# Two decoder blocks on one core: distance in SBUF between moving and next stationary operands, 256 to 448 bytes modulo 512

## The chip, the cores and the metric

The kernel runs on one core of a Trainium2 chip. The metric is the device time of one execution in microseconds (us). Three executions of the kernel before took 3676.75, 3681.95 and 3683.27 us, with a median of 3681.95 us.

## What is computed

The reference runs a residual stream x of 256 tokens by 1024 channels through two blocks, each of two layers, all in float32. A layer of the first block is a mixer, an expert layer and a gate:

```python
xn = rmsnorm(h, norm_mix[l])
z = xn @ w_in[l]                                   # 1024 x 9728
# attention with a window of 128, a short convolution and a gated recurrence, then
y = jnp.einsum('nbsw,nwd->nbsd', branches, w_branch[l])
h = h + jnp.einsum('bsnd,nbsd->bsd', g, y) @ w_out[l]
h = h + peer(rmsnorm(h, norm_ffn[l]), w_peer_q[l], peer_sub_keys[l], peer_u[l], peer_v[l])
h = h + jax.nn.sigmoid(rmsnorm(h, norm_ple[l]) @ w_ple_gate[l]) * (p[l] @ w_ple_proj[l])
```

`peer` picks 16 of 16384 experts for each of 8 heads and token. The kernel computes it densely: all products of the tokens with `peer_u`, a sparse gate, and a product with all of `peer_v`. A layer of the second block projects to 10272 columns, runs a gated delta rule in both directions beside a differential attention, and projects back twice.

## The kernel before, in words

All activations stay in SBUF, channels on the partitions and 256 tokens along the free dimension. Weights come from HBM in pieces of 1 MB into one of three `raw` buffers.

**How a product is made precise.** Most of the products are done in float32r, a float32 form that TensorE takes in one pass, and each operand is split in two: a high part (ScalarE, L167) and the rest (VectorE, L170). `mm3` (L196 to L200) then issues three products for each 128x128 piece of weights: high weights by high x (L198), high weights by low x (L199), low weights by high x (L200). The weights are the stationary operand: 128 columns of float32, 512 bytes in each partition. x is the moving operand: 256 tokens, 1024 bytes in each partition. Every product has a weight load (PEld) of its own.

**Who uses it.** `proj` (L202) calls `mm3` 16 times for 256 output columns, 48 products. `add_rows` (L338) calls it for row blocks of a weight matrix. In the expert layer `u_split` (L902) calls it with rows of `peer_u` as the weights. `v_pair` (from L930, products on L943) turns the roles: activations `ah` and `al` are stationary, 512 columns of split `peer_v` rows (`whi`, `wlo`) are moving. `proj_tok` (L216, products on L226 to L228) also turns them: x is stationary, the weights are moving, 256 columns.

**Products in plain float32.** `u_whole` (L888, products on L898) and the router's projection (L762) use unsplit float32. The profile shows two passes for each of these.

**Where the tiles lie.** Tile pools are placed one after the other in SBUF, in the order in which they are opened: `const`, `state` (the tiles x), `ring` (`raw`, and the split weights `whi` and `wlo`), then the pools of a stage, which are closed and give way to the next stage's: `zp` for the first block's mixer (its split activations are `bh` and `bl`), `peer` (`ah`, `al`), `ple` (`ph`, `pl`, and four weight buffers of its own), `zp2` for the second block's mixer (`bh`, `bl`). `shift(pool, size)` (L75) allocates a dummy tile of `size` bytes in each partition, first in its pool, so that all later tiles of that pool, and of the pools opened after it, lie `size` bytes higher. Nothing reads or writes the dummy. The sizes are `SHIFTS` (L36, one for each layer) and the ring's (L65). The pieces of x within a tile lie 1024 bytes apart and the pieces of weights 512 bytes, so the distance from a moving operand to the stationary one that is loaded meanwhile is the same modulo 512 throughout a stage.

**Order.** The order of instructions on each engine is set when the program is built, by a scheduler with priorities. All weights are issued from SyncE's queue.

Of the kernel before, what the change touches and what calls it, by code (L numbers as in the profile page):

```python
# [32 lines left out]


URGENT = 3000
SHIFTS = {"zp": (320, 96), "zp2": (192, 192), "ple": (192, 448), "peer": (256, 256)}  # L36
SQ_ACT = (2, 5, 7)
HPOOL = ()
WPOOL = 0
# [2 lines left out]
class Tiles:  # L42


    def __init__(self, tiles):
        self.tiles = tiles
# [5 lines left out]
class Ctx:  # L52
# [6 lines left out]
    def __init__(self, ctx, tc):  # L59
        self.tc = tc  # L60
        self.nc = tc.nc
        self.const = ctx.enter_context(tc.tile_pool(name="const", bufs=1))
        self.state = ctx.enter_context(tc.tile_pool(name="state", bufs=1))
        self.ring = ctx.enter_context(tc.tile_pool(name="ring", bufs=1))
        self.shift(self.ring, 256)  # L65
        self.ps = ctx.enter_context(tc.tile_pool(name="ps", bufs=1, space=PSUM))
        self.nax = 0
        self.nsplit = 0
        self.share = 0
        self.nmm = 0  # L70
        self.wide = False
        self.vecs = {}
        self.consts()
# [316 lines left out]
def mixer1(K, a, l, h, norm, prepared, late):  # L390
    tc, nc = K.tc, K.nc
    with ExitStack() as ctx:
        zp = ctx.enter_context(tc.tile_pool(name="zp", bufs=1))
        sm = ctx.enter_context(tc.tile_pool(name="sm", bufs=1))
        K.shift(zp, SHIFTS["zp"][l])

# [289 lines left out]
def peer(K, a, l, pre, xg, row, pool, ctx):  # L686
# [9 lines left out]
    act = pool.tile([128, 128, S], F32, name="act")  # L696
    K.shift(pool, SHIFTS["peer"][l])
    tail = [128 * S]
# [280 lines left out]
def ple(K, a, l, pre, h, hd, out):  # L979

    tc, nc = K.tc, K.nc
    with ExitStack() as ctx:
        p = ctx.enter_context(tc.tile_pool(name="ple", bufs=1))
        K.shift(p, SHIFTS["ple"][l])
        K.dma(h, hd.rearrange("(p k) t -> p k t", k=KT))
# [220 lines left out]
def mixer2(K, a, l, h, pre, c2, fin):  # L1206
    tc, nc = K.tc, K.nc
    cv = pre["vec"]
    with ExitStack() as ctx:
        zp = ctx.enter_context(tc.tile_pool(name="zp2", bufs=1))  # L1210
        K.shift(zp, SHIFTS["zp2"][l])

# [621 lines left out]
```

## Time and profile before

| | |
|---|---|
| runs | 3676.75 to 3683.27 us, median 3681.95 |
| the profiled execution | 3676.36 us |
| its span, first to last instruction | 3674.6 us |
| mean granted TensorE clock | 0.976 of 2.4 GHz |
| busy: TensorE, weight loads, VectorE, ScalarE, GpSimd | 96%, 88%, 71%, 40%, 17% |
| DMA: moved, mean rate | 541.70 MB, 147 GB/s |

The span leaves 1.8 us of the execution's own time for what lies around it. The profiled execution is 5.6 us below the median of the three runs. In the timeline a product's record is longer than the distance to the next one's start, because products overlap in the array; the distance from start to start is called the pitch here.

### The profile page before, as it was taken

Reading aid. Unit: us, or ns where it says so; the run is one execution under the profiler, and the core shown is the slowest. Engines: PE = TensorE matmul, PEld = TensorE weight load, DVE = VectorE, ACT = ScalarE, POOL = GpSimd, SP = SyncE. Lnnn points to the kernel's source line nnn. Section 1 sums busy time; section 2 is a strip of 40 time slices with the busy share of each in tenths; the row PEclk is TensorE's granted clock in tenths of the full one; section 3 lists DMA queues with packets and bytes.
Section 4 is the critical chain, followed back from the end, with each engine's and each line's share of the span. In section 5 each row is a group of like instructions: output and inputs, shape, how many; then the busy total and the mean of one; then the engine's idle time right before and its main releaser. Section 6 shows DMA issues by size and latency. Waiting matters only on the chain. (4 is left out here: it accounts for less than half of the span.)

```text
span 3674.6 us, 60192 instructions
## 1 busy us (share of the span) xinstructions
PE 3520.1 (96%) x23381; PEld 3241.4 (88%) x23381; DVE 2620.0 (71%) x4704; ACT 1476.0 (40%) x2418; POOL 610.8 (17%) x583
## 2 busy tenths in 40 slices
PE   8899999999999999999999999999989999999999
PEld 8898887888888889998888888888888999989999
DVE  6966658876666657775668866666568777698875
ACT  6555211224444446454112134444445344444433
POOL 1200111000000002101121000000033543345441
PEclk9999999999999999999999999999999999999999
DMA  8885766436666567866766446666577544666433
GB/s 172 176 179 138 159 133 134 100 90 184 180 181 180 193 170 159 185 153 148 149 133 120 103 116 182 184 184 185 194 163 139 108 95 103 163 133 124 92 94 117
DMA packets 433976, 541.70 MB, mean 147 GB/s; under 512 B 28665, under 2 KB 392219, under 8 KB 432667
## 3 DMA queue, kind: packets, MB, share of 16 engines
q1 hardware_dynamic: 433690, 537.86, 62.9%
q8 instruction: 183, 3.00, 0.4%
q14 instruction: 103, 0.84, 0.1%
HBM read 530.39 MB, written 6.32 MB: 146 GB/s over the span
## 5 line engine op out<-in xcount | busy, mean ns | idle before, releaser
L170 DVE TENSOR_TENSOR wlo<-raw,whi 128x1024 fp32r<-128x1024 f32 x670 | 861.7, 1291 | 339.2 <-ACT whi L167 323.5
L167 ACT ACTIVATE whi<-raw 128x1024 fp32r<-128x1024 f32 x696 | 728.8, 1051 | 735.7 <-PE mm L199 272.2
L898 PE MATMUL mm<-x,ut 128*128 128x256 f32 x2368 | 546.1, 388 | 1.2 <-ACT act L927 1.2
L200 PE MATMUL mm<-x,wlo 128*128 128x256 f32 x1760 | 509.1, 289 | 11.3 <-DVE wlo L170 11.1
L898 PEld LDWEIGHTS mm<-x,ut 128*128 128x128 f32 x2368 | 455.6, 196 | 65.4 <-ACT act L927 3.7
L198 PE MATMUL mm<-x,whi 128*128 128x256 f32 x1760 | 507.2, 288 | 3.6 <-ACT whi L167 3.6
L199 PE MATMUL mm<-x,whi 128*128 128x256 f32 x1708 | 492.2, 288 | 0.0
L200 PE MATMUL gg<-x,wlo 128*128 128x256 f32 (+1 forms) x1456 | 416.1, 286 | 9.8 <-DVE wlo L170 9.8
L198 PE MATMUL gg<-x,whi 128*128 128x256 f32 (+1 forms) x1456 | 416.3, 286 | 5.7 <-ACT whi L167 5.7
L199 PE MATMUL gg<-x,whi 128*128 128x256 f32 x1400 | 399.0, 285 | 1.0 <-DVE x L303 1.0
L200 PEld LDWEIGHTS mm<-x,wlo 128*128 128x128 f32 x1760 | 342.4, 195 | 14.7 <-DVE wlo L170 13.8
L198 PEld LDWEIGHTS mm<-x,whi 128*128 128x128 f32 x1760 | 342.7, 195 | 10.5 <-issue 5.3
L943 PE MATMUL ax<-wlo,ah 128*128 128x512 f32 x1024 | 318.8, 392 | 20.3 <-DVE wlo L170 20.3
L199 PEld LDWEIGHTS mm<-x,whi 128*128 128x128 f32 x1708 | 332.2, 195 | 1.7 <-issue 0.7
L943 PE MATMUL ax<-whi,al 128*128 128x512 f32 x1024 | 316.7, 391 | 0.0
L200 PEld LDWEIGHTS gg<-x,wlo 128*128 128x128 f32 (+1 forms) x1456 | 280.0, 192 | 11.5 <-DVE wlo L170 11.1
L198 PEld LDWEIGHTS gg<-x,whi 128*128 128x128 f32 (+1 forms) x1456 | 280.1, 192 | 9.1 <-ACT whi L167 6.6
L943 PE MATMUL ax<-whi,ah 128*128 128x512 f32 x1024 | 281.5, 391 | 0.0
L894 DVE STREAM_TRANSPOSE ut<-raw 128x1024 f32<-128x1024 f32 x148 | 182.1, 1237 | 138.1 <-DMA raw<-in_peer_u_dram 111.6
L199 PEld LDWEIGHTS gg<-x,whi 128*128 128x128 f32 x1400 | 269.2, 192 | 2.9 <-DVE x L303 1.1
L943 PEld LDWEIGHTS ax<-wlo,ah 128*128 128x128 f32 x1024 | 190.8, 188 | 68.3 <-DVE wlo L170 29.4
L906 DVE STREAM_TRANSPOSE raw<-raw 128x1024 f32<-128x1024 f32 x108 | 128.1, 1224 | 159.6 <-DMA raw<-in_peer_u_dram 159.6
(534 smaller groups left out, 6705.1 us busy)
## 6 DMA issues: line engine op xcount, KB each, us to landing
raw<-in_w_in_dram SPq DMA_DIRECT2D x592, 256.0 KB
raw<-in_peer_u_dram SPq DMA_DIRECT2D x512, 256.0 KB
raw<-in_peer_v_dram SPq DMA_DIRECT2D x128, 1024.0 KB
raw<-in_w_branch_dram SPq DMA_DIRECT2D x16, 1024.0 KB
raw<-in_w_out_dram SPq DMA_DIRECT2D x16, 1024.0 KB
raw<-in_w_peer_q_dram SPq DMA_DIRECT2D x64, 256.0 KB
raw<-in_w_in_dram SPq DMA_DIRECT2D x64, 128.0 KB
raw<-in_w_branch_dram SPq DMA_DIRECT2D x32, 256.0 KB
```

The source lines that it names most:

```text
L167: nc.scalar.activation(view(hi), src, AF.Copy)
L170: (nc.gpsimd if pool else nc.vector).tensor_tensor(view(lo), src, view(hi).bitcast(F32), ALU.subtract)
L198: t.matmul(out, wh, xh, start=start, stop=False)
L199: t.matmul(out, wh, xl, start=False, stop=False)
L200: t.matmul(out, wl, xh, start=False, stop=stop)
L894: nc.vector.transpose(turned[jh], blk)
L898: nc.tensor.matmul(ps[:, jh], turned[jh][:, k].rearrange("p j c -> p (j c)"), xs[:, k], start=k + jh == 0, stop=k == KT - 1 and jh == 1)
L906: nc.vector.transpose(blk, blk)
L943: nc.tensor.matmul(out[tb][c], lhs[:, j, ts], r[:, c * 512:c * 512 + 512], start=b + j == 0 and lhs is ah and r is vh, stop=b == 63 and j ...
```

## The change

Five numbers for the pools and the ring's one:

```diff
-SHIFTS = {"zp": (320, 96), "zp2": (192, 192), "ple": (192, 448), "peer": (256, 256)}
+SHIFTS = {"zp": (0, 288), "zp2": (384, 384), "ple": (384, 128), "peer": (64, 64)}
...
-        self.shift(self.ring, 256)
+        self.shift(self.ring, 64)
```

The ring moves down by 192 bytes, and with it every pool opened later. `zp` moves by a further -320 and +192 bytes in the two layers, `zp2` by +192, `ple` by +192 and -320, `peer` by -192. The distance (address of the moving operand less address of the stationary one that is loaded next, modulo 512) becomes:

| products | before | after |
|---|---|---|
| x by ring weights (`proj`, `u_split`, `add_rows`) | 256 | 448 |
| `bh`, `bl`, `ph`, `pl` by ring weights | 256 | 448 |
| `peer_v` rows by `ah`, `al` (L943) | 256 | 448 |
| `proj_tok` (L226 to L228) | 256 | 64 |
| the last of the eight low x pieces in `u_split` (tile xl) | 256 | 64 |
| x by the four weight buffers in pool `ple` | 0 | 0 |
| 32-column projection of the second block (L1266), four distances in turn | 256, 384, 0, 128 | 448, 64, 192, 320 |
| decay products (L1473) | 384 | 384 |
| plain float32 (L898, L762) | 256 | 448 |

No instruction, DMA, wait or buffer is added, removed or reordered.

## Rows read from the trace of the kernel before

**Rows 1.** The page, part 1.

```profile
span 3674.6 us, 60192 instructions
...
PE 3520.1 (96%) x23381; PEld 3241.4 (88%) x23381; DVE 2620.0 (71%) x4704; ACT 1476.0 (40%) x2418; POOL 610.8 (17%) x583
```

**Rows 2.** Engines by stage: first mixer, sweep over the experts, second mixer.

```profile
core 0: us, PE busy (x) PEld busy (x) DVE busy (x) ACT busy (x) POOL busy (x), PEclk, DMA share, GB/s
20.00:400.00 380.00, 363.52 (x2916) 351.12 (x2915) 276.38 (x556) 198.49 (x327) 49.64 (x38) 0.98 0.77 167
...
802.00:1322.00 520.00, 508.15 (x2831) 443.43 (x2830) 333.23 (x326) 238.61 (x275) 0.00 (x0) 1.00 0.65 182
...
2735.00:3186.00 451.00, 429.35 (x3432) 416.67 (x3431) 356.47 (x648) 195.42 (x383) 186.03 (x168) 0.97 0.55 119
```

**Rows 3.** TensorE's longest wait in total: engine, line, releaser, us, times, longest.

```profile
PE ax L943 <- DVE wlo L170: 20.3, 21, 1.8
```

**Rows 4.** L198, whole span: PE busy (x count). L199, L200 have this count.

```profile
0.00:3674.60 3674.60, 1244.70 (x4336) 0.98 0.63 147
```

**Rows 5.** L943, whole span.

```profile
0.00:3674.60 3674.60, 716.01 (x3072) 0.98 0.63 147
```

**Rows 6.** L226, whole span. L227 and L228 have this count.

```profile
0.00:3674.60 3674.60, 47.32 (x160) 0.98 0.63 147
```

**Rows 7.** Weight loads and products in u_split: start, length, engine, line.

```profile
999.82 0.28 PE L198 MATMUL gg<-x,whi 128*128 128x256 f32 x1
...
999.82 0.19 PEld L199 LDWEIGHTS gg<-x,whi 128*128 128x128 f32 x1
```

**Rows 8.** Unbroken: distances 256, 0; L943; float32; lower clock (PE, clock, DMA, GB/s).

```profile
1488.10:1585.50 97.40, 97.40 (x813) 1.00 0.82 187
1363.40:1374.90 11.50, 11.50 (x98) 1.00 0.90 168
1212.80:1326.70 113.90, 113.90 (x504) 1.00 0.60 194
425.10:471.70 46.60, 46.60 (x218) 1.00 0.74 141
1341.70:1344.80 3.10, 3.10 (x16) 0.50 0.50 99
```

**Rows 9.** Lower clock, L198 to L200: first and last of 15 starts.

```profile
1341.66 0.41 PE L199 MATMUL mm<-pl,whi 128*128 128x256 f32 x1
...
1344.64 0.41 PE L198 MATMUL gg<-ph,whi 128*128 128x256 f32 x1
```

**Rows 10.** 32-column weights: first and last of 23 starts.

```profile
2812.91 0.28 PE L199 MATMUL gg<-x,whi 128*32 128x256 f32 x1
...
2815.42 0.28 PE L200 MATMUL gg<-x,wlo 128*32 128x256 f32 x1
```

**Rows 11.** After a wait: first, second and ninth start.

```profile
265.00 0.28 PE L199 MATMUL gg<-x,whi 128*128 128x256 f32 x1
265.11 0.28 PE L200 MATMUL gg<-x,wlo 128*128 128x256 f32 x1
...
265.94 0.28 PE L198 MATMUL gg<-x,whi 128*128 128x256 f32 x1
```

**Rows 12.** An uneven run: first, fifth, sixth and last of 16 starts.

```profile
3249.20 0.28 PE L200 MATMUL mm<-x,wlo 128*128 128x256 f32 x1
...
3249.67 0.29 PE L198 MATMUL mm<-x,whi 128*128 128x256 f32 x1
3249.80 0.28 PE L199 MATMUL mm<-x,whi 128*128 128x256 f32 x1
...
3251.00 0.28 PE L200 MATMUL mm<-x,wlo 128*128 128x256 f32 x1
```

## The prediction

> **What bounds the kernel now.** I read the page first. TensorE is busy for 3520.1 of 3674.6 us, 96% [rows 1]. The table by stage then says that this holds in each of the three kinds of long stage: TensorE covers 95 to 98%, and VectorE, the next, 64 to 79% [rows 2]. The waits confirm it: TensorE's longest one, for the low weights of L170, is 20.3 us in total, and it stands idle for only 3674.6 - 3520.1 = 154.5 us [rows 1, 3]. So time is the number of products times their pitch, and the pitch is the only thing that this change can touch.
>
> The busy share hides what the pitch is made of; unbroken stretches show it. A count there takes in one or two products still running at the start. With 256 columns and distance 256, some 812 starts in 97.4 us give a pitch of 120 ns; with 512 columns, some 502 starts in 113.9 us give 227 ns; plain float32 takes 46.6 us for some 216 passes, 216 ns [rows 8]. Where the granted clock is 0.50, the lower of its two levels (1.2 GHz), the same float32r product takes 2.98 us for 14 pitches, 213 ns [rows 8, 9]. Half of that is 106.5 ns. So at 2.4 GHz each product pays 120 - 106.5 = 13.5 ns over what the lower clock promises, and with 512 columns 227 - 213 = 14 ns: a sum per product, not per column. Plain float32 in its slower pass pays 216 - 213 = 3 ns. What else happens once per product is the weight load: that of the next product starts together with the product and runs beside it [rows 7]. The likely reading is that the two streams get in each other's way in SBUF when the moving one runs at full rate. With weights of 32 columns, 22 pitches take 2.51 us, 114 ns [rows 10]: a quarter of the load, about half the excess. Whether the addresses have a part in this is the question.
>
> **The change part by part.** Nothing is added or removed on any engine or queue. Splits, evictions and transfers see addresses moved by multiples of 64 bytes; I cost that at nothing, since they lie beside TensorE with 21% or more of VectorE's time to spare [rows 2]. If a tenth of VectorE's time were added, it would still be covered.
>
> Products: 3 x 4336 from L198 to L200, 3072 from L943 and 3 x 160 from L226 to L228 [rows 4 to 6], 16560 in all. Of these 480 (`proj_tok`) and 108 (tile xl) go to distance 64, 192 in `ple` stay at 0, and 48 have 32 columns. That leaves about 15700 that go from 256 to 448. The mean clock of 0.976 in the table above puts some 5% of the span at the lower level, where a product shows no excess; I take 600 of them off for it. 15100 products x 1 ns = 15.1 us is the lever.
>
> What distance 448 costs no row shows directly, so I bound it. Below: the excess cannot fall under nothing, -13.5 ns, or 15.1 x 13.5 = -204 us; a nearer row is the 32-column one, -6 ns, or -91 us. Above: the largest single pitches are 0.13 us where the mean is 0.12 [rows 12]; as a standing state some 4 ns, +60 us.
>
> Which value? Three things speak. First, distance 0, in `ple`, has 96 starts in 11.5 us, 120 ns as at 256 [rows 8], and the four distances of the 32-column product, multiples of 128, make no difference between its pitches [rows 10]. All float32r rows thus sit on multiples of 128, and 448 does not. Second, the pitch is not fixed at one distance: after a wait, when the weight loads stand in another relation to the products, eight pitches take 265.94 - 265.00 = 0.94 us, 117.5 ns, before it settles at 120 [rows 11]. The settled state is the dear one. A distance changed by 192 bytes shifts that relation by 192 / 1024 of the moving stream, about 20 ns of 106.5. Third, an uneven run with single pitches of 0.13 us has 15 pitches in 1.80 us, 120 ns again [rows 12]; this speaks for a rate that addresses don't change. I take the row nearest to a changed relation, after a wait, and round its gain to 2 ns: 15.1 x 2 = -30 us. Both ends go into the range as far as the chances call for.
>
> The Trainium skill ("TensorE: Matmul & The Clock Gate", "Step-by-step: what each phase is for") says against this that TensorE has two independent read ports in SBUF and that "Loading the next tile's weights doesn't steal SBUF read bandwidth from the running matmul." By that rule the sum is 0; the trace doesn't bear it out as far as the excess of 13.5 ns at full rate goes, but nor does it show that placement decides it.
>
> Plain float32 passes, 2368 on L898 alone, keep 216 ns: they read at half the rate and have 3 ns of excess, so -3 to +1 ns, -7 to +2 us; I take 0. The 588 products that go to 64 count for less than 3 us either way at 4 ns. If products get 2 ns faster, the low weights of L170 are late next: TensorE would meet them some 2% earlier, and VectorE's 64 to 79% leaves room; I take 2 us off the gain and 28 us remain.
>
> The profiled execution is 3676.36 us, 5.6 us under the median of the runs. -28 us gives 3648 for an execution like it, and 3681.95 - 28 = 3654 by the median.
>
> **The rivals.** (a) The forecast: the pitch falls by 1 to 4 ns, 3622 to 3667 us. (b) Nothing changes: the excess belongs to the weight load itself, wherever it lies. For it speak equal pitches at 0 and 256 and the uneven run's mean; against it, that no row has another residue of 128. 3682 us, within 5. The skill's rule of independent ports gives the same time. (c) Slower: at 448 moving and stationary reads meet for longer in the same part of SBUF, in every product from L198 to L943; the pitch becomes 123 ns, 15.1 x 3 = +45 us, 3727 us. It decides from a pitch of 120.5 ns upwards. For it speaks that single pitches of 0.13 us occur; against it, that shorter ones make up for them in that run [rows 12]. (d) Much faster: the two reads part altogether for most of each load, and the pitch falls to the 114 ns of the 32-column weights or under, 3591 us or less. Against it: neither 0 nor 256 does anything like it. (e) The change doesn't do what it says: the distances could come out unequal in some pool; each of the six shifts would have to be wrong, and by the order of the pools they come out as in the table. I give it no chance of its own.
>
> **How the numbers follow.** 0.2%, 7 us, is about what a measurement of this kernel can tell from no change. Chances: (a) 0.36, (d) 0.07, (b) 0.29, (c) 0.28. So faster 0.43, same 0.29, slower 0.28. The likeliest is (a), 3654 us, its own range 3622 to 3667. The range for 8 in 10 takes in (b), the more modest part of (d), down to 3592, and (c) up to a pitch of 123.5 ns, 15.1 x 3.5 = 53 us, 3735.
>
> **What would show it.** Right: the unbroken stretches of `proj` and `u_split` show pitches near 118 ns and L943 near 225, while the `ple` stretch at distance 0 stays at 120 and plain float32 at 216; counts, waits and order stay. Wrong: 120 in all of them (b), 122 or more (c), 114 or less (d). Also wrong would be a change of time with unchanged pitches: then it came from a wait, a transfer or VectorE, which I cost at nothing.

## The result, and the profile after

The changed kernel takes 3621.77 us (median of 4 runs, 3616.71 to 3630.35), the kernel before 3679.35 us (4 runs): 57.6 us less by the medians. Ratios, here and below, are to runs of the kernel before on the same chip, with a 95% interval: 0.9854 (0.9828 to 0.9879) here, 1.5% faster, which is 54 us. The prediction was 3654 us, 28 us faster, with a range from 3592 to 3735. The direction was right and the size was half. The profiled execution is the slowest of the four, 3630.35 us; its span is 46.0 us shorter than that of before.

These rows of the changed kernel's page give its span, busy times and main DMA queue (packets, MB, share of 16 engines):

```profile
span 3628.6 us, 60192 instructions
...
PE 3484.8 (96%) x23381; PEld 3187.9 (88%) x23381; DVE 2623.3 (72%) x4704; ACT 1475.1 (41%) x2418; POOL 604.2 (17%) x583
...
q1 hardware_dynamic: 433690, 537.86, 58.5%
```

Every count is that of [rows 1], and TensorE's share is the same 96%. TensorE's busy time fell by 35.3 us and its idle time, 3628.6 - 3484.8, from 154.5 to 143.8 us. The queue's row is the one to stop at. The same row of the kernel before:

```profile
q1 hardware_dynamic: 433690, 537.86, 62.9%
```

The same packets and bytes took a smaller share of a shorter span. Per packet that is 0.629 x 16 x 3674.6 / 433690 = 85.3 ns before and 0.585 x 16 x 3628.6 / 433690 = 78.3 ns after. Transfers got faster, which a shorter pitch of products does not explain; the experiments separate the two. The stages of [rows 2] have it too, in the last two columns (DMA share, GB/s): more bytes per second at a smaller share.

```profile
20.00:400.00 380.00, 365.43 (x2971) 351.40 (x2970) 278.48 (x557) 199.53 (x331) 49.67 (x38) 0.98 0.71 170
...
802.00:1322.00 520.00, 510.91 (x2825) 437.26 (x2825) 341.14 (x341) 242.48 (x284) 2.99 (x7) 0.99 0.64 188
2735.00:3186.00 451.00, 424.06 (x3426) 410.85 (x3426) 352.63 (x625) 195.97 (x387) 186.50 (x171) 0.96 0.52 124
```

Next come TensorE's waits for low weights. The wait of [rows 3] has almost gone, from 20.3 us to 2.6. The products of `mm3` wait 23.8 us in place of 21.5; before, then after:

```profile
PE mm L200 <- DVE wlo L170: 11.7, 10, 2.6
...
PE gg L200 <- DVE wlo L170: 9.8, 6, 2.4
```

```profile
PE mm L200 <- DVE wlo L170: 14.7, 12, 3.0
...
PE gg L200 <- DVE wlo L170: 9.1, 7, 3.0
...
PE ax L943 <- DVE wlo L170: 2.6, 7, 0.7
```

These are unbroken stretches, as in [rows 8]: two of 256 columns at distance 448 (each with 48 products of `proj_tok`, at 64, which run at the pace of the stretch), then L943 at 448, the `ple` products at 0, plain float32:

```profile
1462.75:1559.76 97.01, 97.01 (x858) 97.01 (x857) 64.78 (x75) 44.97 (x57) 8.30 (x5) 1.00 0.77 197
166.26:239.28 73.02, 73.02 (x621) 73.02 (x621) 50.89 (x126) 36.03 (x45) 0.47 (x1) 1.00 0.83 203
1187.55:1304.92 117.37, 117.37 (x506) 94.07 (x504) 65.28 (x62) 54.87 (x62) 0.00 (x0) 1.00 0.57 188
2663.37:2674.89 11.52, 11.52 (x99) 11.52 (x98) 8.70 (x13) 4.55 (x8) 4.29 (x5) 1.00 0.83 169
1731.45:1778.94 47.49, 47.49 (x223) 41.81 (x222) 33.94 (x106) 7.21 (x15) 10.67 (x14) 1.00 0.70 152
```

By the starts inside them these are 856 pitches of 113.3 ns, 620 of 117.8, 503 of 233.3, 96 of 120.0 and 220 of 215.9 (a count also takes in a product or two that still ran at the start). So 256 columns went from 120 to one of **two** settled values, 113.3 or 117.8 ns at one and the same distance; L943 went the other way, from 227 to 233 ns; distance 0 and plain float32 stayed.

To see what each part is worth, take the start-to-start times of products in program order. An interval under 130 ns (240 ns for 512 columns and plain float32) counts as unbroken; the mean of these times the number of intervals is the part "at pitch", and what longer intervals have above that mean is the part "beyond", waits and stretches at the lower clock. How intervals between two kinds are counted moves the parts at pitch by up to some 1%. The float32 column takes in the intervals from a float32 product to one of another kind; without them its part beyond is 21.8, 16.3, 15.4 and 18.9 us, from top to bottom. In us, for the four kernels that matter:

| kernel | 256 columns, at pitch / beyond | L943, at pitch / beyond | plain float32, at pitch / beyond | span |
|---|---|---|---|---|
| before | 1583.0 / 92.0 | 697.4 / 28.5 | 634.5 / 48.6 | 3674.6 |
| after | 1525.3 / 108.9 | 715.7 / 6.9 | 634.6 / 41.0 | 3628.6 |
| raw buffers moved alone (below) | 1582.9 / 92.9 | 697.4 / 4.8 | 634.6 / 36.7 | 3638.3 |
| distances alone (below) | 1520.0 / 114.0 | 715.7 / 22.9 | 634.6 / 49.1 | 3652.6 |

From before to after the pitch gives 57.7 us and takes 18.3 back at L943; beyond it, 16.9 us more are spent among the 256-column products and 21.6 and 7.6 less in the other two. That is -51.7 us; the rest of the span's change, +5.7 us, lies in other kinds of products and between kinds. The 16.9 us are not all waits. Of the intervals between 256-column products, those at the lower clock number 338 instead of 263, some 8 us of it; intervals of 240 ns and more, waits, make some 6 us; the rest is shorter gaps.

### The profile page after: what moved, and what is told of

Same layout as the page of the kernel before. It is cut to its first block, busy times and chain, and to the rows that moved or that the text cites. A ratio compares the mean times of both kernels' runs of the same rounds, so it can differ in the third digit from the quotient of the medians.

```text
span 3628.6 us, 60192 instructions
## 1 busy us (share of the span) xinstructions
PE 3484.8 (96%) x23381; PEld 3187.9 (88%) x23381; DVE 2623.3 (72%) x4704; ACT 1475.1 (41%) x2418; POOL 604.2 (17%) x583
## 3 DMA queue, kind: packets, MB, share of 16 engines
q1 hardware_dynamic: 433690, 537.86, 58.5%
## 5 line engine op out<-in xcount | busy, mean ns | idle before, releaser
L170 DVE TENSOR_TENSOR wlo<-raw,whi 128x1024 fp32r<-128x1024 f32 x670 | 862.7, 1293 | 325.8 <-ACT whi L167 311.3
L167 ACT ACTIVATE whi<-raw 128x1024 fp32r<-128x1024 f32 x696 | 728.7, 1051 | 709.0 <-PE mm L199 271.9
L898 PE MATMUL mm<-x,ut 128*128 128x256 f32 x2368 | 542.6, 386 | 1.2 <-ACT act L927 1.2
L200 PE MATMUL mm<-x,wlo 128*128 128x256 f32 x1760 | 506.6, 288 | 14.4 <-DVE wlo L170 14.1
L898 PEld LDWEIGHTS mm<-x,ut 128*128 128x128 f32 x2368 | 453.0, 194 | 64.3 <-ACT act L927 3.9
L198 PE MATMUL mm<-x,whi 128*128 128x256 f32 x1760 | 504.4, 287 | 3.3 <-ACT whi L167 3.3
L199 PE MATMUL mm<-x,whi 128*128 128x256 f32 x1708 | 488.9, 286 | 0.0
L200 PE MATMUL gg<-x,wlo 128*128 128x256 f32 (+1 forms) x1456 | 410.5, 282 | 9.3 <-DVE wlo L170 9.1
L198 PE MATMUL gg<-x,whi 128*128 128x256 f32 (+1 forms) x1456 | 410.9, 282 | 4.9 <-ACT whi L167 4.9
L199 PE MATMUL gg<-x,whi 128*128 128x256 f32 x1400 | 393.6, 281 | 1.3 <-DVE x L303 1.3
L200 PEld LDWEIGHTS mm<-x,wlo 128*128 128x128 f32 x1760 | 340.8, 194 | 18.2 <-DVE wlo L170 17.2
L198 PEld LDWEIGHTS mm<-x,whi 128*128 128x128 f32 x1760 | 340.7, 194 | 10.7 <-issue 5.6
L199 PEld LDWEIGHTS mm<-x,whi 128*128 128x128 f32 x1708 | 331.6, 194 | 1.9 <-issue 0.7
L943 PE MATMUL ax<-wlo,ah 128*128 128x512 f32 x1024 | 323.0, 396 | 2.6 <-DVE wlo L170 2.6
L943 PE MATMUL ax<-whi,al 128*128 128x512 f32 x1024 | 321.4, 395 | 0.0
L200 PEld LDWEIGHTS gg<-x,wlo 128*128 128x128 f32 (+1 forms) x1456 | 276.3, 190 | 11.7 <-DVE wlo L170 11.3
L943 PE MATMUL ax<-whi,ah 128*128 128x512 f32 x1024 | 286.6, 395 | 0.0
L198 PEld LDWEIGHTS gg<-x,whi 128*128 128x128 f32 (+1 forms) x1456 | 275.7, 189 | 8.2 <-ACT whi L167 5.6
L199 PEld LDWEIGHTS gg<-x,whi 128*128 128x128 f32 x1400 | 265.9, 190 | 3.5 <-DVE x L303 1.4
L943 PEld LDWEIGHTS ax<-wlo,ah 128*128 128x128 f32 x1024 | 190.2, 187 | 54.8 <-DVE wlo L170 9.2
L943 PEld LDWEIGHTS ax<-whi,al 128*128 128x128 f32 x1024 | 191.7, 187 | 47.1
```

What stands on the lines that cost most here:

```text
L167: nc.scalar.activation(view(hi), src, AF.Copy)
L170: (nc.gpsimd if pool else nc.vector).tensor_tensor(view(lo), src, view(hi).bitcast(F32), ALU.subtract)
L198: t.matmul(out, wh, xh, start=start, stop=False)
L199: t.matmul(out, wh, xl, start=False, stop=False)
L200: t.matmul(out, wl, xh, start=False, stop=stop)
L898: nc.tensor.matmul(ps[:, jh], turned[jh][:, k].rearrange("p j c -> p (j c)"), xs[:, k], start=k + jh == 0, stop=k == KT - 1 and jh == 1)
```

## The experiments

The change alters the ring's shift and all eight numbers of `SHIFTS` (two for each of four pools, not five in all). There are two theories: the pitch does it all, or the pitch does part and the absolute addresses, which the ring's shift moves along with the distances, do the rest.

**L943 left at 256.** The change with `peer` at its old distance:

```diff
-... "peer": (64, 64)}
+... "peer": (256, 256)}
```

> The changed kernel, but pool peer keeps its 256 bytes of shift: the products of L943 and the tile xl stay at distance 256, all other products go to 448. Theory A (each pair's distance sets its own pitch): L943 goes back from 233 to 227 ns, 3072 x 6.3 ns = 19 us off the changed kernel's time at most; as its waits for the low weights shrank from 20.3 to under 3 us in the changed kernel, part of that comes back as waiting, so 3605 to 3622 us, ratio to before 0.979 to 0.985. The 256-column pitch stays near 115 ns. Theory B (the gain came from absolute addresses, by way of the transfers): same as the changed kernel, 0.985, with L943 at any pitch.

3603.74 us, ratio 0.9824 (0.981 to 0.9837), some 11 us below the changed kernel's 0.9854; the two intervals just overlap (that one begins at 0.9828). Its unbroken stretches, the same pieces of program as the first three above:

```profile
1448.70:1545.82 97.12, 97.12 (x859) 97.12 (x858) 64.88 (x75) 45.09 (x57) 8.29 (x5) 1.00 0.76 197
165.54:235.58 70.04, 70.04 (x620) 70.04 (x619) 50.60 (x126) 36.18 (x45) 0.42 (x1) 1.00 0.91 211
1177.48:1291.53 114.05, 114.05 (x505) 94.41 (x504) 65.23 (x62) 54.94 (x62) 0.00 (x0) 1.00 0.59 194
```

L943's 503 pitches are 114.05 us again, 226.7 ns, so its 233 came from its distance. The second row is the surprise: the same 618 pitches at the same distance that took 117.8 ns in the changed kernel take 113.3 here.

**L943 alone at 448.** The kernel before with `peer` at (64, 64):

```diff
-... "peer": (256, 256)}
+... "peer": (64, 64)}
```

> The kernel before with pool peer's shift at 64 alone: only L943 (distance 448) and xl (64) move. Theory A: L943 at 233 ns, 256-column products at 120 ns; 19 us more of products, less the waits in front of L943 (20.3 us) that this can take up: 0 to +19 us, ratio 1.000 to 1.005. Theory B: the ring does not move, so the time of before, L943 at 227 ns.

3680.92 us, ratio 1.0026 (1.0016 to 1.0035), 9.5 us slower by the before of that chip. The stretch and the wait:

```profile
1208.56:1325.92 117.36, 117.36 (x505) 94.07 (x504) 65.27 (x62) 54.86 (x62) 0.00 (x0) 1.00 0.59 188
```

```profile
PE ax L943 <- DVE wlo L170: 8.1, 19, 1.3
```

3072 products x 6 ns are 18 us, and half of it shows: L943 had waited 20.3 us for VectorE, and slower products leave 8.1 us of that. A pitch is worth its whole count only where no wait ahead of the products takes up part of it.

**Every address moved, every distance kept.** The kernel before with one dummy at the foot of `state`, so that the ring and what follows move by as much, modulo 512, as in the change, and the x tiles with them:

```diff
         self.ring = ctx.enter_context(tc.tile_pool(name="ring", bufs=1))
+        self.shift(self.state, 320)
```

> The kernel before with 320 bytes of shift ahead of the tiles x, so that x, ring and all pools lie as the ring does in the changed kernel modulo 512 (raw buffers at a multiple of 512), but every distance stays 256. Theory A: nothing changes, 3680 us within 7, 256-column pitch 120 ns, L943 227 ns, even if the transfers take a smaller share of their queues. Theory B: the changed kernel's time, ratio 0.985, and a DMA share near 58.5% instead of 62.9%.

3638.68 us, ratio 0.9919 (0.9905 to 0.9934). Every pitch is that of before (119.8, 227.3 and 216 ns) and 31 us are gone. The queue, and VectorE's wait for `peer_u` (L906 of the other kernels is L907 here):

```profile
q1 hardware_dynamic: 433690, 537.86, 57.9%
```

```profile
DVE raw L907 <- DMA raw<-in_peer_u_dram: 120.7, 54, 3.6
```

In the kernel before that wait is 159.6 us:

```profile
DVE raw L906 <- DMA raw<-in_peer_u_dram: 159.6, 54, 4.7
```

This settles the theory of the pitch alone: it falls. The addresses alone do not reach the changed kernel's 0.9854 either. What moved that transfers could see? The `raw` buffers lay 192 bytes past a multiple of 512 and lie on one now.

**The raw buffers alone.** `raw` is the ring's first tile. With the ring's shift at 64 and a dummy of 192 bytes behind `raw`, only `raw` moves (the call of `raw_tile` places the three buffers ahead of the dummy):

```diff
-        self.shift(self.ring, 256)
+        self.shift(self.ring, 64)
+        self.raw_tile()
+        self.shift(self.ring, 192, "shift3")
```

> Only the three raw buffers, into which nearly all transfers write, move from 192 to 0 bytes past a multiple of 512; every other tile and every distance of the float32r products stays as before. Theory (the transfers' destination): pitches stay at 120 and 227 ns, the share of the main DMA queue falls from 62.9% to about 58%, VectorE waits less for peer_u (L906 of before, 159.6 us, to about 120) and the time is 0.992 of before, as where everything moved together. Rival (it was the other tiles that moved along: operands that TensorE, VectorE and ScalarE read): share 62.9%, ratio 0.998 to 1.002.

3638.59 us, ratio 0.9906 (0.9891 to 0.9921), as much as with everything moved. The queue's share, TensorE's wait at L943 (L945 here), VectorE's for `peer_u`, and the unbroken stretches:

```profile
span 3638.3 us, 60192 instructions
...
q1 hardware_dynamic: 433690, 537.86, 57.9%
```

```profile
PE ax L945 <- DVE wlo L172: 1.7, 4, 0.7
```

```profile
DVE raw L908 <- DMA raw<-in_peer_u_dram: 119.4, 54, 3.6
```

```profile
1465.51:1568.70 103.19, 103.19 (x862) 103.19 (x861) 65.42 (x75) 45.95 (x57) 8.29 (x5) 1.00 0.72 187
1189.36:1303.40 114.04, 114.04 (x505) 94.42 (x504) 65.24 (x62) 54.94 (x62) 0.00 (x0) 1.00 0.59 194
```

860 pitches of 120.0 and 503 of 226.7: TensorE's products are those of before. A packet takes 0.579 x 16 x 3638.3 / 433690 = 77.7 ns instead of 85.3. VectorE and ScalarE, which read `raw`, keep their times (splits of low parts 1291 ns before and 1290 here, of high parts 1051 in both). The chain of work, as the waits show it: `peer_u` lands earlier, VectorE's transposes and splits run earlier, and L943 no longer waits for low weights. The table above puts the gain where that chain ends: 23.7 us beyond the pitch at L943 and 11.9 in plain float32, which on L898 also feeds on `peer_u` (6.0 between products of L898, 5.5 where a product of L772 follows one).

**The distances alone.** The changed kernel with `raw` put back to 192 bytes past a multiple of 512:

```diff
-        self.shift(self.ring, 64)
+        self.shift(self.ring, 256)
+        self.raw_tile()
+        self.shift(self.ring, 320, "shift3")
```

> The distances of the changed kernel, with the raw buffers back at 192 bytes past a multiple of 512. Theory (two separate causes that add): queue share 62.9%, pitch of the 256-column products 115 ns, L943 233 ns; the ratio to before is that of the changed kernel over that of the moved buffers, 0.9854/0.9919 = 0.993, so 3655 us (3645 to 3665). Rival 1 (the faster products only pay once the transfers are faster, since stages wait for weights): pitches as said, ratio 0.998 to 1.002. Rival 2 (the pitch does all and the buffers matter only where distances are 256): ratio 0.985.

3654.97 us, ratio 0.9953 (0.9939 to 0.9966), queue share back up:

```profile
q1 hardware_dynamic: 433690, 537.86, 63.1%
```

The expected 0.993 came from the run with everything moved, whose interval is wide enough to allow for the difference; with `raw` alone, 0.9906 x 0.9953 = 0.9859 against 0.9854 for the change. So within the intervals the two parts add up: 34 us from the transfers' destination, 18 from the distances. Of these the table tells that the 256-column pitch gave 63.0 us, and the sum kept less than a third: 18.3 went to L943, and 22.0 came back beyond the pitch among the 256-column products. Of the 22.0, some 12 us are products at the lower clock, 377 such intervals instead of 263, and some 8 us are waits. The waits that can be named there, for the low weights of `mm3`, went from 11.7 and 9.8 us, by 7.8 in all, to the following (L202 and L172 are L200 and L170 of the others):

```profile
PE mm L202 <- DVE wlo L172: 17.1, 12, 3.0
...
PE gg L202 <- DVE wlo L172: 12.2, 7, 3.1
```

**Where raw may lie.** Two more kernels move `raw` alone, to 128 and 64 bytes past a multiple of 512 (ring shift 192 and dummy 64, as below, or both 128):

```diff
-        self.shift(self.ring, 256)
+        self.shift(self.ring, 192)
+        self.raw_tile()
+        self.shift(self.ring, 64, "shift3")
```

> The kernel before with the raw buffers alone moved, now to 128 bytes past a multiple of 512 (0 and 256 gave a queue share of 58%; 192, 352 and 480 gave 63%). Theory (what counts is whether a row of a transfer begins on a multiple of 256 bytes): 63%, ratio 0.998 to 1.002. Rival (a multiple of 128 is enough): 58%, ratio 0.991. Pitches 120 and 227 in both.

> The same with the raw buffers 64 bytes past a multiple of 512. Theory (multiples of 256): 63%, ratio 0.998 to 1.002. Rival (the share grows with the distance from the multiple, so 64 is half as slow): 60%, ratio 0.995.

At 128: 3643.93 us, ratio 0.9891 (0.986 to 0.9923). At 64: 3679.47 us, ratio 0.9995 (0.998 to 1.0011). The queue's rows, 128 first:

```profile
q1 hardware_dynamic: 433690, 537.86, 59.4%
```

```profile
q1 hardware_dynamic: 433690, 537.86, 62.1%
```

So the expected multiple of 256 fell at one end: 128 is nearly as good as 0. The expected text counts a kernel at 352 as slow; that sweep's ring shift of 96 puts `raw` 32 bytes past a multiple of 512, not 352. With the sweeps below, packets take 77.7 ns at 0 and at 256, 79.8 at 128, 85.2 at 32, 84.0 at 64, 85.3 at 192 and 85.9 at 480.

**Three sweeps for the pitch.** Each places x, the mixers' split activations and L943 at other distances (x 416, 480 and 192; `raw` then lies at 32, 480 and 256). The lines of shifts and of the ring, one pair for each:

```diff
+SHIFTS = {"zp": (32, 224), "zp2": (480, 288), "ple": (352, 96), "peer": (32, 128)}
+        self.shift(self.ring, 96)
...
+SHIFTS = {"zp": (160, 480), "zp2": (96, 128), "ple": (416, 160), "peer": (448, 384)}
+        self.shift(self.ring, 32)
...
+SHIFTS = {"zp": (288, 128), "zp2": (256, 352), "ple": (128, 384), "peer": (320, 192)}
+        self.shift(self.ring, 320)
```

> Several distances in one kernel: x by ring weights 416; bh, bl 480 and 384 in the first block's two layers, 32 and 352 in the second's; L943 480 and 384. Theory A: each group has a settled pitch of its own in an unbroken stretch, 113 to 120 ns for 256 columns; near 448 (416, 480) I expect 113 to 118 ns, at 384 and the far ones 120. If only the residue modulo 128 counts, 32, 352, 416 and 480 pair up (32 with 416, 352 with 480) and 384 equals 256. Theory B: one pitch for all groups.

> One look for pitches: products of the mixers at distances 96, 128, 160 and 192, x elsewhere at 480, L943 at 64 in the first layer and 128 in the second, raw buffers 480 bytes past a multiple of 512. Theory (the pitch follows the distance alone, in steps of 64 bytes or so): 96 gives 120 as it did for the products by tokens, 128 to 192 give 120 like 256; L943 lies between 227 and 233. Rival (a symmetric curve about 0: 64 bytes on either side are as good): 64 at L943 is 233 as at 448. Theory of the destination: a multiple of 512 alone is fast, share 62.9%; its rival (a few bytes off is only a little slow): share 60%.

> One look for pitches: x at distance 192 everywhere, products of the mixers at 224, 288, 320 and 416, L943 at 192 in the first layer and 320 in the second, raw buffers 256 bytes past a multiple of 512. Theory (the 256-column curve repeats every 256 bytes, from 192 having given 114 as 448 did): x at 192 is 115, 224 is 118 as 480, 288 is 117 as 32, 320 is 117 as 64, 416 is 118; its rival (192 was fast for bh alone) gives x some 120. L943 at 192 is 233 and at 320 is 229. Destination: if any multiple of 256 is fast the queue's share is 58% and the time 3625 or so, if only multiples of 512 are, 63% and 3655.

They have one run each, too few to tell small differences: 3671.97, 3669.21 and 3619.51 us, beside medians of 3670.09, 3672.89 and 3667.88 of before. Only the last has `raw` on a multiple of 128, and the queue's row says so:

```profile
q1 hardware_dynamic: 433690, 537.86, 58.2%
```

Mean unbroken pitches over all these kernels, in ns, by the distance modulo 256:

| distance modulo 256 | 0 | 32 | 64 | 96 | 128 | 160 | 192 | 224 |
|---|---|---|---|---|---|---|---|---|
| measured at | 0, 256 | 32, 288 | 64, 320 | 96, 352 | 128, 384 | 160, 416 | 192, 448 | 224, 480 |
| 256 columns | 120 | 117 | 116 to 118 | 119 to 121 | 119 | 118 | 114 to 116 | 118 |
| L943, 512 columns | 227 | | 229 | | 231 | | 233 | 233 |

Distances that differ by 256 give the same pitch, within the spread shown, wherever both were measured. For 256 columns the value at 64 rests in the main on `proj_tok`, whose products in the changed kernel ran at 113.4 or 117.8 ns, whichever pace the stretch around them had. Three expectations fell: 160 and 192 are not at 120 but at 118 and 114, 352 is not like 480, and `raw` at 256 is as fast as at 0. L943 rises by some 2 ns for each 64 bytes; the last run shows it in two layers, 192 and then 320, 503 pitches of 233.3 and 228.9:

```profile
1184.40:1301.76 117.36, 117.36 (x506) 94.06 (x504) 65.26 (x62) 54.88 (x62) 0.00 (x0) 1.00 0.57 188
2498.74:2613.87 115.13, 115.13 (x506) 94.46 (x504) 65.27 (x62) 54.87 (x62) 0.00 (x0) 1.00 0.56 192
```

The best place for 256 columns, 192 or 448, is the worst for 512.

**Which of the two settled pitches.** In the changed kernel the first half of `u_split` runs at 113 in 48 of 54 blocks, and the second at 118 in all; with L943 left at 256 it is the other way round in all 54. The change of pace comes at the product that reads tile xl, the only one at another distance. Changed kernel: first product after L943, that of xl, first product of the second half, its xl:

```profile
933.02 0.28 PE L198 MATMUL mm<-x,whi 128*128 128x256 f32 x1
...
935.52 0.28 PE L199 MATMUL mm<-xl,whi 128*128 128x256 f32 x1
...
935.76 0.28 PE L198 MATMUL mm<-x,whi 128*128 128x256 f32 x1
...
938.35 0.28 PE L199 MATMUL mm<-xl,whi 128*128 128x256 f32 x1
```

The same four with L943 at 256 (xl then lies at 256 too):

```profile
923.67 0.28 PE L198 MATMUL mm<-x,whi 128*128 128x256 f32 x1
...
926.26 0.28 PE L199 MATMUL mm<-xl,whi 128*128 128x256 f32 x1
...
926.50 0.28 PE L198 MATMUL mm<-x,whi 128*128 128x256 f32 x1
...
929.02 0.28 PE L199 MATMUL mm<-xl,whi 128*128 128x256 f32 x1
```

22 pitches take 2.50 and then 2.59 us in the first (113.6 and 117.7 ns), 2.59 and then 2.52 in the second. Two kernels followed. The first puts xl at 448 as well, with L943 at 256:

```diff
-                        pool.tile([128, S], F32R, name="xl", tag="oh", bufs=2))
+                        pool.tile([128, S + 64], F32R, name="xl", tag="oh", bufs=2)[:, 48:48 + S])
```

> The shifts of the changed kernel, L943 left at 256, and the one xl tile that lay at another distance (64, or 256 where L943 stays) put at 448. Theory (two settled pitches; a product at another distance throws the run of products from 113 to 118 ns): in peer_u's split products both halves run at 113, the second half's 24 products of 54 blocks gain 4.5 ns each, some 6 us: ratio 0.981 where it was 0.9824 without this. Rival (the upper pitch belongs to the second half's own addresses, which hold turned weights of other buffers): the second half stays at 118 and the ratio is 0.9824.

3610.59 us, ratio 0.9828 (0.9814 to 0.9842): no gain. The theory had both halves at 113; both are at 118. Without xl's step nothing changes pace inside a block, but after L943 all 54 runs start at 118 and stay there (mean 117.75). So in `u_split` xl's product does switch the pace, downwards where it lies at 256 and the run began high, which this kernel shows by its absence, and upwards at 64 in the changed kernel, where no kernel without it was run. The theory had the upward step alone. The second kernel adds a switch early: the first xl tile at 256, one product in 24.

```diff
+        if at == 1:
+            return self.state.tile([128, S + 128], dtype, name="x", tag="x1", bufs=1)[:, 80:80 + S]
         return self.state.tile([128, S], dtype, name="x", tag=f"x{at}", bufs=1)
```

> As the kernel before this (distances 448, L943 at 256, the last xl at 448), but the first xl tile lies at distance 256, so that one product in 24 (48 in the projections) stands 256 from its successor's weights. Theory (a product at 256 sets the lower settled pitch, as the last xl at 256 did from the first to the second half of peer_u's products, where L943 stayed): from the first such product on the runs stay at 113; both halves of the split products mean 113.5 to 114, the share of quads at the upper pitch falls from about 40% to under 15%, and 3,000 products or more gain 4.4 ns: 0.978 to 0.980 against 0.982. Rival (such a product only toggles between the two): halves and quads stay about as mixed as they are and the ratio is 0.982 to 0.984, a little up for some 400 products at 120.

3606.79 us, ratio 0.9821 (0.9807 to 0.9834): no gain again. In `u_split` both halves do run low (mean 114.8, the switching products included), near what the theory had. Over the whole kernel it falls: of all groups of four unbroken 256-column intervals in a row, 37% have a mean of 117 to 118.5 ns, the upper pitch, where the kernel before this one has 40%, and the mean pitch does not fall (115.6 after 115.4). Here are the two long stretches of 256 columns, the same pieces of program as the first two shown for the changed kernel:

```profile
1455.73:1557.02 101.29, 101.29 (x861) 101.29 (x861) 65.42 (x75) 45.64 (x57) 8.31 (x5) 1.00 0.75 190
166.18:239.21 73.03, 73.03 (x621) 73.03 (x621) 50.91 (x126) 36.09 (x45) 0.47 (x1) 1.00 0.85 203
```

The 860 pitches of the first have a mean of 117.8; the changed kernel ran them at 113.3. In the projections two such products follow each other at three products' distance, and the pace behind them is the one ahead of them. So distance 256 does not simply set the lower pace, and in `u_split` it does not simply toggle either. What decides stays open, as does what picks the pace when products start after a wait: in the stretch of 618 products, which comes before the pool `peer` is opened, no address differs between the changed kernel (117.8) and the one with L943 at 256 (113.3). Each kernel has one trace, so it is also not shown whether the pace there differs from one execution to the next.

Of the kernels with several runs the three with L943 at 256 and the rest at 448 are the fastest, 0.9821 to 0.9828, not told apart from each other. The plainest of them, `SHIFTS` of the change with `peer` at (256, 256), is the version to keep.

## Why the prediction was right or wrong

**What bounds the kernel.** Right as far as it went: 96% TensorE, before and after. But "time is the number of products times their pitch, and the pitch is the only thing that this change can touch" did not hold. 154.5 us of idle time and the time beyond the pitch were left out of that sentence, and the 34 us of the transfers came from there.

**Transfers at nothing.** This is the step that failed: "Splits, evictions and transfers see addresses moved by multiples of 64 bytes; I cost that at nothing, since they lie beside TensorE". The splits did stay (L170 and L167 keep their durations), the transfers did not: 85.3 to 77.7 ns a packet, 34 us with `raw` moved alone. Nor did they lie wholly beside TensorE. [rows 3] had the mark, 20.3 us at L943 for weights whose chain begins with a transfer, and the prediction read it as too small to matter, not as time that a faster transfer could give back. The text did say what would show this ("a change of time with unchanged pitches"), and the kernel with all distances kept is that case. The Trainium skill has a rule that bears on it ("DMA: Bandwidth & Descriptors", "How a descriptor splits into AXI transactions"): by the vendor's account, when a descriptor does not start on a multiple of 256 bytes, its first transaction starts at the boundary below, and the bytes before its start still cost. The page speaks of bytes that are fetched; whether it holds for the buffer that a transfer fills, it doesn't say. The packet times agree with it for 0 and 256 against 32, 64, 192 and 480, and differ at 128, where 79.8 ns and a ratio of 0.9891 stand with the aligned ones. Why 128 is enough stays open.

**Two nanoseconds off the pitch.** That distance moves the pitch was right: it moves with the distance, stays where all addresses move and every distance is kept, and plain float32 and distance 0 stayed as forecast. The reading behind it, two streams in each other's way in SBUF, no run shows. The sizes were wrong. For 256 columns -2 was taken and -4.4 measured (119.8 to 115.4, a mix of 113.3 and 117.8). For L943 the same -2 was taken, "near 225", and it is +6. One term for both was the mistake: they share the distance but not the length of the moving operand, and the sweeps give them different curves, with 192 the lowest for one and the highest for the other. By the prediction's own term, 12,000 of its products gain 4.4 ns and 3072 lose 6. The row it chose, eight pitches of 117.5 ns after a wait [rows 11], turned out close to the upper of the two settled values; that this is more than coincidence is not shown.

**Two microseconds off for late weights.** The thing was right, the size not, and another term was missing. 16.9 us of the 57.7 came back beyond the pitch (22.0 of 63.0 with the distances alone). The named waits for the low weights of `mm3` grew by 2.3 us (7.8 with the distances alone), all waits by some 6 (8). The larger part, some 8 us (12), is more products at the lower clock, which the prediction held at the 600 it took off. Intervals at the lower clock number 338 (377) there, and 245 to 307 in the kernels whose 256-column pitch is the old one; why is not shown. VectorE's 64 to 79% are means over a stage; where a block waits for its low weights, faster products only reach the wait sooner.

**Nearer than its parts, by chance.** With the distances alone the time falls by 18 us. The forecast of 28 for just this was nearer than its parts, since the gain in pitch was taken too small, L943's sign was wrong, and the return was taken too small. The rival that nothing changes had its support in the Trainium skill's rule of two independent read ports ("TensorE: Matmul & The Clock Gate", "Step-by-step: what each phase is for"). The same products take 120 ns at distance 256 and 113.3 or 117.8 at 448, so where the operands lie does matter; whether reads in SBUF are the reason, no run shows.

## What to carry to other kernels

A shift at the foot of a stack of buffers moves two things, distances between operands and absolute addresses; before pricing one, ask which engine or queue sees the other, and separate them with a second dummy. In this kernel the buffers that transfers fill do best on multiples of 128 bytes, and products of different lengths want a distance of their own; try both. When a kernel is bound by TensorE, look at its few longest waits as well as at its pitch: 20 us in 3675, behind a chain that starts with a transfer, were the mark of the larger part of this gain.

## What the runs showed of the hardware that was not expected

- Packets whose destination `raw` lies at 0, 128 or 256 bytes modulo 512 take 77.7 to 79.8 ns, at 32, 64, 192 or 480 84.0 to 85.9. At 0, 64, 128 and 192 nothing else differed; at 32, 256 and 480 the distances did too.
- A product of 256 columns in float32r with its own weight load has a pitch that depends on the distance modulo 256 bytes: 120 ns at 0, some 115 at 192. At 512 columns it is 227 at 0 and 233 at 192. Plain float32 passes stay at 216 at all five distances tried (192, 256, 416, 448, 480).
- At distance 448 two pitches are stable, 113.3 and 117.8 ns, for hundreds of products in a row; in `u_split` one product at another distance switches between them, in the projections a pair of such products did not.
